# A decoder block's first stage: x turned by products with a diagonal, weights loaded ahead of parameters, units interleaved by k

## The chip, the cores and the metric

The kernel runs on one core of a Trainium2 chip. Five engines work at the same time, each in the order of its own queue: PE (TensorE, matrix products), DVE (VectorE), ACT (ScalarE), POOL (GpSimd) and SP (SyncE, which issues all loads and stores here). The metric is the time of one execution on the device in microseconds (us), lower is better. Before the change three runs gave 1006.0, 1007.21 and 1008.55 us, so a median of 1007.21 us.

## The reference

One decoder block on x with 1024 positions and 1024 channels, all float32. x is divided by its root mean square per position and scaled by a gain per channel; one large projection feeds two branches (an mLSTM with four heads and a diagonal state-space model, S5), which are gated, merged and projected again. The stage that matters here is the first:

```python
def rmsnorm(x, g):
    xf = x.astype(jnp.float32)
    y = xf * lax.rsqrt(jnp.mean(xf * xf, axis=-1, keepdims=True) + NORM_EPS)
    return (y * g.astype(jnp.float32)).astype(x.dtype)

xn = rmsnorm(h, norm_pre_g[l])
proj = xn @ w_in[l]
u_a, z_a, o_a, i_a, f_a, u_b, z_b, g_pre = jnp.split(proj, split_points, axis=-1)
g = jax.nn.sigmoid(g_pre.astype(jnp.float32)).astype(h.dtype)
```

## The kernel before

Every float32 product of the projections is made of three faster ones: an operand a is split into a high part `ah` (ACT writes it, rounded to fp32r) and a low part `al` = a - ah (DVE or POOL), and `dot3` (L179 to L182) adds `ah.bh`, `ah.bl` and `al.bh` in one bank of PSUM. For the weights, `split_w` (L133) does this: `wr` is the raw tile of a load, `wh` and `wl` its parts (L140, L142). For x the parts are `xh[k]` and `xl[k]`, one pair for each of the eight blocks k of 128 channels, with the channels on partitions and the 1024 positions along the row; `HS[0]` and `HS[1]` are the two halves of 512 positions.

x arrives with positions on partitions, in eight tiles `xt` of 128 positions. So it must be normalised and turned. `norm_x` (L266) does the first: ACT squares and sums a row (L269), POOL forms the mean plus epsilon and raises it to the power -1/2 (L270, L271), DVE multiplies the tile with it in place (L272). Turning is a PE transpose against the identity, 128x128 at a time: for the first half of positions eight banks `pts[0]` to `pts[7]`, one for each k, receive four tiles each (L342); for the second half `trans_x` (L279) takes one bank for each k. `evac_x` (L274) then writes `xh` (ACT, times the gain `gpre`) and `xl` (DVE).

A unit is one block of 128 output channels by 512 positions: 24 products into one bank, over k = 0 to 7. `g_unit(i, m, hf)` computes the gates, and tanh of the bank goes to `tg` on ACT and from there to memory. The first stage runs g_unit(0, 0, 0) and g_unit(0, 1, 0), turns the second half, and runs g_unit(0, 0, 1) and g_unit(0, 1, 1). Then the eight `ub` units follow. PSUM has two groups of banks, `pp` (3, for units) and `pm` (5, `mbank()`); the eight `pts` take all of them, so the first unit's bank is that of `pts[0]` and comes free only when `xh[0]` and `xl[0]` have been written.

The order on each engine is the order in which the Python code issues instructions. What sets it here:

- Loads on SP: four x tiles, seven small loads of parameters into `prow` (gain, convolution, head gain and others, L326), the first weights (`fetch()`), four x tiles. Each load uses one of eight semaphores in turn, so the ninth waits for the first to land, the tenth for the second, and so on.
- `pump()` takes raw weights that have been fetched and issues their split; `take(key)` hands a split pair to a unit and pumps the next one ahead. So `take(("g", 0))` in the first unit also issues the split of the weights for `ub` 0, ahead of that unit's tanh.
- 24 transposes of the identity (L334) run on PE before the first tile is ready; nobody reads what they write.

Of the kernel before, what the change touches and what calls it, by code (L numbers as in the profile page):

```python
# [36 lines left out]
def hybrid_block(ctx, tc, x, norm_pre_g, w_in, conv_w, conv_b, w_q, w_k, w_v, b_i, b_f, head_g,  # L37
# [227 lines left out]

    def norm_x(t, xt):  # L266
        s = ssx[:, t:t + 1]
        jk = xp.tile([P, D], F32, tag="junk", bufs=2, name="junk")
        A.activation(jk, xt, AF.Square, accum_out=s)  # L269
        PL.tensor_scalar(s, s, 1.0 / D, EPS, op0=ALU.mult, op1=ALU.add)  # L270
        PL.tensor_tensor(s, s, halfm[:, 0:1], op=ALU.pow)  # L271
        V.tensor_scalar(xt, xt, s, None, op0=ALU.mult)  # L272

    def evac_x(hf, k, pt):  # L274
        A.activation(xh[k][:, HS[hf]], pt, AF.Copy, scale=gpre[:, k:k + 1])
        V.scalar_tensor_tensor(xl[k][:, HS[hf]], pt, gpre[:, k:k + 1],  # L276
                               xh[k][:, HS[hf]].bitcast(F32), op0=ALU.mult, op1=ALU.subtract)

    def trans_x(hf, k, xts):  # L279
        pt = mbank()  # L280
        for t in range(4):
            PE.transpose(pt[:, t * P:(t + 1) * P], xts[t][:, k * P:(k + 1) * P], ident)
        evac_x(hf, k, pt)


    def spill_tanh(o, dst):
# [1 line left out]
        A.activation(t, o, AF.Tanh, scale=0.5)  # L288
# [23 lines left out]


    xts = [load_x(t) for t in range(4)]
    NPAR = 72
    prow = xp.tile([NPAR, P], F32, tag="prow", bufs=1, name="prow")
    r0 = 0
    for src, n in ((norm_pre_g, 8), (conv_w, 32), (conv_b, 8), (head_g, 8), (skip_a, 8), (b_glu, 4),
                   (D_skip, 4)):
# [12 lines left out]
    pts = [bank() if k < 3 else mbank() for k in range(KT)]
    for i in range(24):
        PE.transpose(pts[i % 4][:, :P], ident, ident)  # L334
    for t in range(4):
        norm_x(t, xts[t])
        if t == 3:
            pt = pts[7][:, 3 * P:3 * P + NPAR]
            PE.transpose(pt, prow, ident[:NPAR, :NPAR])
            V.tensor_copy(par, pt)  # L340
# [2 lines left out]
    hg, sk, bgl, dsk = par[:, 48:56], par[:, 56:64], par[:, 64:68], par[:, 68:72]
    pump(lambda: [evac_x(0, k, pts[k]) for k in range(2)])
    for k in range(2, KT):
        evac_x(0, k, pts[k])
    V.tensor_scalar(par[:, 48:64], par[:, 48:64], 0.25, None, op0=ALU.mult)
# [1109 lines left out]
```

## Time and profile before

| what | value |
| --- | --- |
| runs | 1006.0, 1007.21, 1008.55 us |
| the profiled execution | 1006.37 us |
| its span from the first to the last instruction | 1004.3 us |
| mean granted clock of PE | 0.993 |
| PE, DVE, ACT, POOL busy | 976.7, 615.5, 351.1, 154.6 us |
| share of PE in the chain that ended last | 83% |
| products `pp<-xh,wh` at L180, 128x512 | 768, 401 ns each by the records |

The profiled execution's time is 2.1 us more than the span, which lies around it. A row of the timeline holds the start in us, the duration in us, the engine, the line, the operation, the tile written and those read, the shape and the count; in brackets stands how long the engine sat idle before, and what ended that. Products are pipelined: the records of two in succession overlap, and the distance of their starts is what one costs. A row of the windows holds the stretch, then busy time and count of PE, PE's weight loads, DVE, ACT and POOL, the granted clock of PE, the share of the DMA engines and GB/s. In the page's table of 40 slices PE is busy 7 tenths in the first slice, 9 or more in 38, and 7 in the last; the clock is 8 tenths in the first slice and 9 or more in the others.

### The profile page before, as it was taken

What the parts mean: (1) busy time and instruction counts of PE and PEld (TensorE: products, weight loads), DVE (VectorE), ACT (ScalarE), POOL (GpSimd) and SP (SyncE); (2) the same over time, 40 slices, a digit from 0 to 9 for tenths busy, and PEclk for the clock granted to TensorE, in tenths of its full rate; (3) what the DMA queues carried; (4) which work ended last, traced back from release to release, by engine and by line L of the source; (5) the groups of instructions that cost most, each with busy time, mean ns of one, the idle gap of its engine ahead of it and who ended that gap; (6) DMA issues with size and microseconds to landing.
All of it is one profiled execution on the core that took longest, in us unless ns stands there. A gap on an engine that the chain in (4) does not pass through costs nothing.

```text
span 1004.3 us, 15220 instructions
## 1 busy us (share of the span) xinstructions
PE 976.7 (97%) x5617; PEld 840.9 (84%) x5617; DVE 615.5 (61%) x1400; ACT 351.1 (35%) x696; POOL 154.6 (15%) x210
## 2 busy tenths in 40 slices
PE   7999999999999999999999999999999999999997
PEld 6888888788778788978988899889987888779997
DVE  4426496686952854254677477747774888675226
ACT  7322131233032531223544355435543452223311
POOL 4001000000000000012112232223221311343001
PEclk8999999999999999999999999999999999999999
DMA  7344221333056447314433354336436796783504
GB/s 253 94 153 157 90 95 36 93 111 109 17 177 187 170 156 253 107 42 126 138 121 131 95 174 131 135 86 184 132 121 215 248 318 202 271 301 118 189 1 168
DMA packets 115449, 148.31 MB, mean 148 GB/s; under 512 B 19080, under 2 KB 71472, under 8 KB 115376
## 3 DMA queue, kind: packets, MB, share of 16 engines
q1 hardware_dynamic: 115376, 147.35, 45.7%
q8 instruction: 44, 0.72, 0.3%
q14 instruction: 29, 0.24, 0.1%
HBM read 100.88 MB, written 46.43 MB: 147 GB/s over the span
## 4 chain that ended last, share of the span: by engine, by line
PE 83%; DVE 10%; DMA 3%; issue 2%; ACT 1%; SPq 0%; POOL 0%; DVEq 0%; POOLq 0%; ACTq 0%
PE pp L180 22%; PE pp L182 22%; PE pp L181 22%; PE pm L182 4%; PE pm L180 4%; PE pm L181 3%; DVE wl L142 1%; PE pm L1084 1%; DMA wr<-in_w_in_dram 1%; DVE zt L439 1%; PE pm L1007 1%; DMA xt<-in_x_dram 1%; DMA ft<-t_d 1%; PE pm L661 1%; DVE ec_r L439 1%
## 5 line engine op out<-in xcount | busy, mean ns | idle before, releaser
L180 PE MATMUL pp<-xh,wh 128*128 128x512 f32 x768 | 307.6, 401 | 3.2 <-DVE xl L276 2.4
L182 PE MATMUL pp<-xh,wl 128*128 128x512 f32 x768 | 305.0, 397 | 4.4 <-DVE wl L142 4.4
L181 PE MATMUL pp<-xl,wh 128*128 128x512 f32 x768 | 304.7, 397 | 0.0
L182 PEld LDWEIGHTS pp<-xh,wl 128*128 128x128 f32 x768 | 145.0, 189 | 41.0 <-DVE wl L142 6.2
L180 PEld LDWEIGHTS pp<-xh,wh 128*128 128x128 f32 x768 | 145.0, 189 | 39.3 <-DVE xl L276 2.7
L181 PEld LDWEIGHTS pp<-xl,wh 128*128 128x128 f32 x768 | 145.1, 189 | 32.7
L142 DVE TENSOR_TENSOR wl<-wr,wh 128x1024 fp32r<-128x1024 f32 (+2 forms) x71 | 83.4, 1211 | 46.3 <-ACT wh L140 41.7
L140 ACT ACTIVATE wh<-wr 128x1024 fp32r<-128x1024 f32 (+2 forms) x76 | 73.2, 1008 | 40.8 <-PE pm L181 30.7
L182 PE MATMUL pp<-wh,ml 128*128 128x256 f32 x256 | 72.8, 284 | 0.5 <-POOL ml L1363 0.5
L180 PE MATMUL pp<-wh,mh 128*128 128x256 f32 x256 | 72.9, 285 | 0.0
L180 PE MATMUL pp<-wh,xh 128*128 128x256 f32 (+1 forms) x256 | 72.0, 281 | 0.0
L181 PE MATMUL pp<-wl,mh 128*128 128x256 f32 x256 | 71.9, 281 | 0.0
L288 ACT ACTIVATE tg<-pp 128x512 f32<-128x512 f32 x32 | 19.1, 599 | 151.1 <-PE pp L182 75.2
L181 PE MATMUL pp<-wl,xh 128*128 128x256 f32 (+1 forms) x256 | 71.8, 280 | 0.0
L182 PE MATMUL pp<-wh,xl 128*128 128x256 f32 (+1 forms) x256 | 71.8, 280 | 0.0
L182 PEld LDWEIGHTS pp<-wh,ml 128*128 128x128 f32 x256 | 48.1, 188 | 0.7 <-POOL ml L1363 0.7
L181 PEld LDWEIGHTS pp<-wl,mh 128*128 128x128 f32 x256 | 48.6, 190 | 0.1
L180 PEld LDWEIGHTS pp<-wh,mh 128*128 128x128 f32 x256 | 48.4, 189 | 0.2 <-ACT mh L1362 0.2
L181 PEld LDWEIGHTS pp<-wl,xh 128*128 128x128 f32 x256 | 48.2, 188 | 0.2
L180 PEld LDWEIGHTS pp<-wh,xh 128*128 128x128 f32 x256 | 48.1, 188 | 0.2
L182 PEld LDWEIGHTS pp<-wh,xl 128*128 128x128 f32 x256 | 48.0, 187 | 0.0
L981 POOL TENSOR_TENSOR hll<-t2k,hlh 128x512 fp32r<-128x512 f32 x16 | 20.8, 1297 | 166.2 <-ACT hlh L980 89.4
(395 smaller groups left out, 1731.5 us busy)
## 6 DMA issues: line engine op xcount, KB each, us to landing
wr<-in_w_in_dram SPq DMA_DIRECT2D x48, 512.0 KB
t_d<-tg SPq DMA_DIRECT2D x32, 256.0 KB
xt<-in_x_dram SPq DMA_DIRECT2D x8, 512.0 KB
aux<-t_d SPq DMA_DIRECT2D x16, 256.0 KB
gb_d<-aux SPq DMA_DIRECT2D x16, 256.0 KB
so_d<-sow SPq DMA_DIRECT2D x32, 128.0 KB
sz_d<-t2k SPq DMA_DIRECT2D x16, 256.0 KB
cs_d<-t2k SPq DMA_DIRECT2D x16, 256.0 KB
```

The lines of the kernel that those rows point to most:

```text
L140: A.activation(hi, raw, AF.Copy)
L142: eng.tensor_tensor(wl[:, k0:k0 + n, c0:c0 + w], raw, hi.bitcast(F32), op=ALU.subtract)
L180: PE.matmul(o, lh, rh, start=first, stop=False)
L181: PE.matmul(o, lh, rl, start=False, stop=False)
L182: PE.matmul(o, ll, rh, start=False, stop=last)
L288: A.activation(t, o, AF.Tanh, scale=0.5)
L439: V.tensor_tensor(o, a, b, op=op)
L661: PE.matmul(o[NS * b2:NS * (b2 + 1), g * P:(g + 1) * P], q["wt"][:, ri, g, NS * b2:NS * (b2 + 1)], ut[b][:, 2 * g + b2, :], start=True, st ...
L981: PL.tensor_tensor(lo, acc, hi.bitcast(F32), op=ALU.subtract)
L1007: PE.matmul(pm[:, 256 * k:256 * k + 256], wt[:, e, 256 + P * k:256 + P * k + P], wt[:, e, 0:256], start=e == 0, stop=e == 1)
L1084: PE.matmul(sc[:, :P], k_[:, m, sl], q_[:, m, sl], start=m == 0, stop=m == 1)
```

## The change

In `norm_x` the tile itself is left as it is. The mean moves from POOL to DVE, and DVE writes a diagonal `dg` (identity times 1/rms, 128x128) in place of the scaled tile. The turn becomes a true float32 product `xt.T @ dg` (`turn_x`), which turns and scales at once. One tile of the first four (t = 2) is squared on DVE.

The gain gets a load of its own, `grow`, and its own transpose; it and the first weights are loaded ahead of the second four x tiles and of the other parameters, whose transpose comes after both pairs of units. The first weights are split by hand, in pieces of two, two and four blocks of k. More dummy transposes (`warm`) are issued: 30 ahead, and 2, 2 and 10 behind the tiles 0, 1 and 2.

The units of a half run as a pair (`g_pair`): two banks, k by k, six products for each k. The turning of the second half lies among them, and the norms of the second four tiles among the writing of `xh` and `xl`. The split of the next weights (`pump()`) comes after both pairs.

```diff
-    def norm_x(t, xt):
+    def norm_x(t, xt, vec):
...
-        A.activation(jk, xt, AF.Square, accum_out=s)
-        PL.tensor_scalar(s, s, 1.0 / D, EPS, op0=ALU.mult, op1=ALU.add)
+        if vec:
+            V.scalar_tensor_tensor(jk, xt, 1.0, xt, op0=ALU.mult, op1=ALU.mult, accum_out=s)
+        else:
+            A.activation(jk, xt, AF.Square, accum_out=s)
+        V.tensor_scalar(s, s, 1.0 / D, EPS, op0=ALU.mult, op1=ALU.add)
         PL.tensor_tensor(s, s, halfm[:, 0:1], op=ALU.pow)
-        V.tensor_scalar(xt, xt, s, None, op0=ALU.mult)
+        dgs[t] = xp.tile([P, P], F32, tag="dg", bufs=8, name="dg")
+        V.tensor_scalar(dgs[t], ident, s, None, op0=ALU.mult)
+
+    def turn_x(pt, xt, t, k):
+        PE.matmul(pt[:, (t % 4) * P:(t % 4 + 1) * P], xt[:, k * P:(k + 1) * P], dgs[t], start=True, stop=True)
...
+    def g_pair(i, hf, before):
+        tick()
+        wh, wl = cur["g"]
+        o = [bank(), bank()]
+        steps = [(0, 0), (0, 1), (1, 0), (1, 1)] + [(m, k) for k in range(2, KT) for m in range(2)]
+        for m, k in steps:
+            if m == 0:
+                before(k)
+            mc = slice(m * P, (m + 1) * P)
+            dot3(o[m], wh[:, k, mc], wl[:, k, mc], xh[k][:, HS[hf]], xl[k][:, HS[hf]], k, k == 0, k == KT - 1)
+        for m in range(2):
+            g_done(i, m, hf, o[m])
...
     xts = [load_x(t) for t in range(4)]
+    SY.dma_start(grow, norm_pre_g[0].rearrange("(k p) -> k p", p=P))
+    fetch()
+    xts2 = [load_x(t) for t in range(4, 8)]
...
-    fetch()
-    xts2 = [load_x(t) for t in range(4, 8)]
...
-    for i in range(24):
-        PE.transpose(pts[i % 4][:, :P], ident, ident)
+    warm(30)
     for t in range(4):
-        norm_x(t, xts[t])
+        norm_x(t, xts[t], t == 2)
+        if t == 1:
+            PE.transpose(pts[7][:, 3 * P:3 * P + KT], grow, ident[:KT, :KT])
+            V.tensor_copy(gpre, pts[7][:, 3 * P:3 * P + KT])
         for k in range(KT):
-            PE.transpose(pts[k][:, t * P:(t + 1) * P], xts[t][:, k * P:(k + 1) * P], ident)
+            turn_x(pts[k], xts[t], t, k)
+        if t < 3:
+            warm((2, 2, 10)[t])
...
+    A.activation(wh[:, 0:2], ra[:, 0:2], AF.Copy)
+    A.activation(wh[:, 2:4], ra[:, 2:4], AF.Copy)
+    sub(V, slice(0, 2), ra[:, 0:2])
+    for k in range(KT):
+        evac_hi(0, k, pts[k])
+        evac_lo(0, k, pts[k])
+        if k == 1:
+            sub(V, slice(2, 4), ra[:, 2:4])
+            A.activation(wh[:, 4:8], rb, AF.Copy)
+            sub(PL, slice(4, 8), rb)
+        if k >= 3 and k < 7:
+            norm_x(k + 1, xts2[k - 3], False)
+    pending.append(fetch)
+    g_pair(0, 0, lambda k: k < 6 or trans_x(1, k - 6, xts2))
+    g_pair(0, 1, lambda k: k > 5 or trans_x(1, k + 2, xts2))
+    pump()
+    pt = mbank()[:, :NPAR]
+    PE.transpose(pt, prow, ident[:NPAR, :NPAR])
+    V.tensor_copy(par, pt)
...
-    run(unit(lambda: g_unit(0, 0, 0)))
-    run(unit(lambda: g_unit(0, 1, 0)))
-    for k in range(KT):
-        trans_x(1, k, xts2)
-    for m in range(2):
-        run(unit(lambda: g_unit(0, m, 1)))
     prep.close()
```

Three places in the engines' order show what moved. First, PE in the prologue. Before, from the third tile's transposes to the first product of a unit (L342 the transposes of a tile, L339 that of the parameters, L180 a unit's product):

```order
L342 MATMUL pp<-ident,xt 128x128 x3
L342 MATMUL pm<-ident,xt 128x128 x5
L339 MATMUL pm<-ident,prow 128x72
L342 MATMUL pp<-ident,xt 128x128 x3
L342 MATMUL pm<-ident,xt 128x128 x5
L180 MATMUL pp<-xh_96,wh 128x512
```

Now, from behind tile 0's products to tile 3's (L281 the products with `dg`, L368 the dummies, L374 the transpose of the gain):

```order
L368 MATMUL pp<-ident 128x128 x2
L374 MATMUL pm<-ident,grow 128x8
L281 MATMUL pp<-dg,xt 128x128 x3
L281 MATMUL pm<-dg,xt 128x128 x5
L368 MATMUL pp<-ident 128x128 x2
L281 MATMUL pp<-dg,xt 128x128 x3
L281 MATMUL pm<-dg,xt 128x128 x5
L368 MATMUL pp<-ident 128x128 x3
L368 MATMUL pm<-ident 128x128 x4
L368 MATMUL pp<-ident 128x128 x3
L281 MATMUL pp<-dg,xt 128x128 x3
L281 MATMUL pm<-dg,xt 128x128 x5
```

Dummies and the gain's transpose now stand between the tiles, ten of them between tile 2 and tile 3; the parameters' transpose has moved to behind both pairs.

Second, DVE from its first instruction to the first low part of x (L275 the mean, L278 the diagonal, L272 the square of tile 2, L389 a weight split, L287 a low part). Now:

```order
L275 TENSOR_SCALAR ssx<-ssx 128x1
L278 TENSOR_SCALAR dg<-ident,ssx 128x128
L375 COPY par<-pm 128x8
L272 SCALAR_TENSOR_TENSOR junk,ssx<-xt 128x1024
L275 TENSOR_SCALAR ssx<-ssx 128x1
L278 TENSOR_SCALAR dg<-ident,ssx 128x128
L275 TENSOR_SCALAR ssx<-ssx 128x1
L278 TENSOR_SCALAR dg<-ident,ssx 128x128
L389 TENSOR_TENSOR wl<-wr,wh 128x512
L287 SCALAR_TENSOR_TENSOR xl_104<-pp,par,xh_96 128x512
```

Before, there stood four scalings of a tile, the copy of all parameters, a whole weight split and then the first low part; the copy of the gain now stands ahead of tile 2's square.

Third, ACT around the end of the stage (L140 the high part of weights, L269 a Square, L288 or L300 the tanh of a gate unit, L275 or L284 a high part of x, L374 or L429 the copy of a `ub` unit). Before:

```order
L269 ACTIVATE junk,ssx<-xt 128x1024 x4
L140 ACTIVATE wh<-wr 128x1024 x2
L288 ACTIVATE tg<-pp 128x512 x2
L275 ACTIVATE xh_96<-pm,par 128x512
L275 ACTIVATE xh_97<-pm,par 128x512
```

Now:

```order
L284 ACTIVATE xh_102<-pm,par 128x512
L284 ACTIVATE xh_103<-pm,par 128x512
L300 ACTIVATE tg<-pp 128x512 x2
L140 ACTIVATE wh<-wr 128x1024 x4
L429 COPY uc<-pp 128x8x64 x4
```

The two high parts of the weights for `ub` 0 stood ahead of the first pair's tanh; now they are the first two of the four behind the second pair's tanh.

More of the change, by code (lines that the diff above doesn't have):

```diff
@@ L264, in load_x, with evac_hi, evac_lo @@
         return xt
-    def norm_x(t, xt):
+    dgs = {}
+    def norm_x(t, xt, vec):
         s = ssx[:, t:t + 1]
         jk = xp.tile([P, D], F32, tag="junk", bufs=2, name="junk")
[L269 to L274, printed above, removed]
+        if vec:
[3 more added lines that the diff above has]
+        V.tensor_scalar(s, s, 1.0 / D, EPS, op0=ALU.mult, op1=ALU.add)
+        PL.tensor_tensor(s, s, halfm[:, 0:1], op=ALU.pow)
+        dgs[t] = xp.tile([P, P], F32, tag="dg", bufs=8, name="dg")
+        V.tensor_scalar(dgs[t], ident, s, None, op0=ALU.mult)
+    def turn_x(pt, xt, t, k):
+        PE.matmul(pt[:, (t % 4) * P:(t % 4 + 1) * P], xt[:, k * P:(k + 1) * P], dgs[t], start=True, stop=True)
+    def evac_hi(hf, k, pt):
         A.activation(xh[k][:, HS[hf]], pt, AF.Copy, scale=gpre[:, k:k + 1])
+    def evac_lo(hf, k, pt):
         V.scalar_tensor_tensor(xl[k][:, HS[hf]], pt, gpre[:, k:k + 1],
@@ L281, in trans_x @@
         for t in range(4):
-            PE.transpose(pt[:, t * P:(t + 1) * P], xts[t][:, k * P:(k + 1) * P], ident)
-        evac_x(hf, k, pt)
+            turn_x(pt, xts[t], 4 * hf + t, k)
+        evac_hi(hf, k, pt)
+        evac_lo(hf, k, pt)
     def spill_tanh(o, dst):
@@ L291, in hybrid_block, with g_done @@
     cur = {}
+    def g_done(i, m, hf, o):
+        ct = 2 * i + m
+        dst = (t1_d if ct < 8 else t2_d)[(ct % 8) * P:(ct % 8 + 1) * P, HS[hf]]
+        spill_tanh(o, dst)
+    def g_pair(i, hf, before):
[10 more added lines that the diff above has]
+            g_done(i, m, hf, o[m])
     def g_unit(i, m, hf):
@@ L297, in g_unit @@
         proj_cm(o, cur["g"], m * P, xh, xl, HS[hf])
-        ct = 2 * i + m
-        dst = (t1_d if ct < 8 else t2_d)[(ct % 8) * P:(ct % 8 + 1) * P, HS[hf]]
-        spill_tanh(o, dst)
+        g_done(i, m, hf, o)
     def zb_unit(i, m, hf):
@@ L314, in hybrid_block @@
     xts = [load_x(t) for t in range(4)]
-    NPAR = 72
+    grow = xp.tile([KT, P], F32, tag="grow", bufs=1, name="grow")
+    SY.dma_start(grow, norm_pre_g[0].rearrange("(k p) -> k p", p=P))
+    fetch()
+    xts2 = [load_x(t) for t in range(4, 8)]
+    NPAR = 64
     prow = xp.tile([NPAR, P], F32, tag="prow", bufs=1, name="prow")
     r0 = 0
-    for src, n in ((norm_pre_g, 8), (conv_w, 32), (conv_b, 8), (head_g, 8), (skip_a, 8), (b_glu, 4),
-                   (D_skip, 4)):
+    for src, n in ((conv_w, 32), (conv_b, 8), (head_g, 8), (skip_a, 8), (b_glu, 4), (D_skip, 4)):
         src = src[0]
@@ L327, in hybrid_block, with warm @@
         r0 += n
-    fetch()
-    xts2 = [load_x(t) for t in range(4, 8)]
-    par = main.tile([P, 80], F32, name="par")[:, 0:NPAR]
-    gpre, cw, cb = par[:, 0:8], par[:, 8:40].rearrange("p (j k) -> p j k", j=4), par[:, 40:48]
+    par = main.tile([P, 80], F32, name="par")
+    gpre, par = par[:, 64:72], par[:, 0:NPAR]
+    cw, cb = par[:, 0:32].rearrange("p (j k) -> p j k", j=4), par[:, 32:40]
+    hg, sk, bgl, dsk = par[:, 40:48], par[:, 48:56], par[:, 56:60], par[:, 60:64]
     pts = [bank() if k < 3 else mbank() for k in range(KT)]
-    for i in range(24):
-        PE.transpose(pts[i % 4][:, :P], ident, ident)
+    def warm(n):
+        for i in range(n):
+            PE.transpose(pts[i % 7][:, 3 * P:], ident, ident)
@@ L335, in hybrid_block @@
+    warm(30)
     for t in range(4):
-        norm_x(t, xts[t])
[L337 to L340, printed above, removed]
-        for k in range(KT):
-            PE.transpose(pts[k][:, t * P:(t + 1) * P], xts[t][:, k * P:(k + 1) * P], ident)
[L343 to L346, printed above, removed]
@@ L347, in hybrid_block @@
-    V.tensor_scalar(par[:, 48:64], par[:, 48:64], 0.25, None, op0=ALU.mult)
-    V.tensor_scalar(bgl, bgl, 0.5, None, op0=ALU.mult)
-    for t in range(4):
-        norm_x(t + 4, xts2[t])
-    run(unit(lambda: g_unit(0, 0, 0)))
-    run(unit(lambda: g_unit(0, 1, 0)))
-    for k in range(KT):
-        trans_x(1, k, xts2)
-    for m in range(2):
-        run(unit(lambda: g_unit(0, m, 1)))
+        norm_x(t, xts[t], t == 2)
+        if t == 1:
+            PE.transpose(pts[7][:, 3 * P:3 * P + KT], grow, ident[:KT, :KT])
+            V.tensor_copy(gpre, pts[7][:, 3 * P:3 * P + KT])
@@ new lines, in hybrid_block, with sub @@
+        for k in range(KT):
+            turn_x(pts[k], xts[t], t, k)
+        if t < 3:
+            warm((2, 2, 10)[t])
+    key, kt, ncol, raws = raw_q.popleft()
+    wh = wp.tile([P, kt, ncol], F32R, tag="wh", name="wh")
+    wl = wp.tile([P, kt, ncol], F32R, tag="wl", name="wl")
+    ra, rb = raws[0][2], raws[1][2]
+    cur["g"] = (wh, wl)
+    assert key == ("g", 0)
+    def sub(eng, ks, raw):
+        eng.tensor_tensor(wl[:, ks], raw, wh[:, ks].bitcast(F32), op=ALU.subtract)
+    A.activation(wh[:, 0:2], ra[:, 0:2], AF.Copy)
@@ L357, in hybrid_block @@
+    pump()
+    pt = mbank()[:, :NPAR]
+    PE.transpose(pt, prow, ident[:NPAR, :NPAR])
+    V.tensor_copy(par, pt)
+    V.tensor_scalar(par[:, 40:56], par[:, 40:56], 0.25, None, op0=ALU.mult)
+    V.tensor_scalar(bgl, bgl, 0.5, None, op0=ALU.mult)
     prep.close()
```

## The prediction

> **What bounds the kernel now.** I read the page's busy table first, then the chain that ended last, then the first 50 us piece by piece.
>
> ```profile
> PE 976.7 (97%) x5617; PEld 840.9 (84%) x5617; DVE 615.5 (61%) x1400; ACT 351.1 (35%) x696; POOL 154.6 (15%) x210
> ```
>
> PE (TensorE) is busy 97% of the 1004.3 us span and the chain of waits lies on it for 83%. The change touches only the start, and everything behind it (DVE's work on the S5 parameters too) is released by PE in program order. So a microsecond at which the first `ub` unit starts later is a microsecond of time; I see nothing later that would absorb it. The question is when that unit starts and runs on, now and then. The chain in order of time begins thus:
>
> ```profile
> 2.16 6.21 DMA xt<-in_x_dram
> 8.38 4.00 DMA wr<-in_w_in_dram
> 12.40 1.07 ACT wh L140
> 13.49 1.23 DVE wl L142
> 14.72 0.67 DVE xl L276
> 15.44 0.79 PE pp L180
> ```
>
> The fourth x tile lands at 8.38, only then are the first weights issued, they land at 12.40, are split in two steps, and PE's first product starts at 15.44. The windows give the granted clock (the last figure but two of a row):
>
> ```profile
> 14.00:15.00 1.00, 0.00 (x0) 0.00 (x0) 1.00 (x2) 1.00 (x3) 0.00 (x0) 0.87 1.01 410
> 21.00:22.00 1.00, 1.00 (x4) 0.76 (x4) 0.75 (x1) 1.00 (x5) 0.72 (x2) 0.72 0.34 115
> ```
>
> During PE's pause the clock falls to half (from the 0.87, at about 14.7), and it comes back at about 21.6 (the 0.72). PE's own rows show the price and the ends of the stage:
>
> ```profile
> 15.44 0.79 PE L180 MATMUL pp<-xh,wh 128*128 128x512 f32 x1 [2.42 <-DVE xl L276]
> 29.51 2.76 PE L282 MATMUL pm<-ident,xt 128*128 128x128 f32 x23
> 33.45 0.47 PE L180 MATMUL pp<-xh,wh 128*128 128x512 f32 x1
> 44.50 0.39 PE L182 MATMUL pp<-xh,wl 128*128 128x512 f32 x1
> 44.73 0.40 PE L180 MATMUL pp<-xh,wh 128*128 128x512 f32 x1
> ```
>
> From 33.45 to 44.73, 48 products take 11.28 us (0.235 each). The same 48 of the first half take 14.07 us (15.44 to 29.51), so the cold clock costs 2.8 us. The 32 transposes between take 3.94 us (0.123 each). At 44.73 the `ub` unit follows without a gap.
>
> **The change, part by part.** *Turning by a product.* A float32 product of 128x128 by 128x128 occurs at L701 and L702; each shows as two records:
>
> ```profile
> 177.98 0.40 PE L182 MATMUL pp<-xh,wl 128*128 128x512 f32 x1
> 178.21 0.39 PE L701 MATMUL pm<-ut,m 128*128 128x128 f32 x2
> 181.56 0.39 PE L702 MATMUL pm<-ss__1532,vs 128*128 128x128 f32 x2
> ```
>
> From the first start to the last lie 15 products in 3.35 us: 0.223 each. So the 32 of the second half cost 7.14 us on PE, where 32 transposes cost 3.94: **+3.2 us**. They lie between products of the units, but PE does one thing at a time, so nothing hides them.
>
> *When the first product starts.* Tile 0 before:
>
> ```profile
> 4.58 1.06 ACT L269 ACTIVATE junk<-xt 128x1024 f32<-128x1024 f32 x1 [2.52 <-DMA xt<-in_x_dram]
> 5.82 0.19 POOL L270 TENSOR_SCALAR ssx<-ssx 128x1 f32<-128x1 f32 x1 [4.40 <-ACT junk L269]
> 5.86 1.06 ACT L269 ACTIVATE junk<-xt 128x1024 f32<-128x1024 f32 x1
> 6.09 0.55 POOL L271 TENSOR_TENSOR ssx<-ssx,halfm 128x1 f32<-128x1 f32 x1
> 6.68 0.75 DVE L272 TENSOR_SCALAR xt<-xt,ssx 128x1024 f32<-128x1024 f32 x1 [6.68 <-POOL ssx L271]
> 20.13 0.17 DVE L347 TENSOR_SCALAR par<-par 128x16 f32<-128x16 f32 x1
> ```
>
> The mean now runs on DVE, a small instruction as at 20.13 (0.17); the power stays (0.55). The diagonal, 128 wide, lies between 0.17 (16 wide) and 0.75 (1024 wide); on a line between them 0.23. With the old hand-overs of 0.05 to 0.08 it is ready at 6.9. Tile 0's eight products run from 6.95 to 8.73, two dummies and the transpose of the gain row end at 9.06 (this row, queued right behind the fourth x tile, should land near 8.4), tile 1's products at 10.84, two more dummies at 11.05. Tile 2's square is on DVE, behind the gain copy that waits for that transpose: 9.3, copy 0.2, then a 1024-wide instruction with two inputs (1.23, as wl L142 above), mean, power and diagonal about 1.05: ready at 11.8. Its products run from 11.85 to 13.63. Then the **ten dummies** (0.107 each, from the pitch of the warm ones: 4.59 to 5.02 is four) stand in PE's queue ahead of tile 3 until 14.7, although tile 3's diagonal is ready at 12.9, one such chain behind tile 2's. Tile 3's first product ends its bank at about 15.1.
>
> ```profile
> 4.59 0.27 PE L334 MATMUL pm<-ident 128*128 128x128 f32 x1
> 5.02 0.27 PE L334 MATMUL pm<-ident 128*128 128x128 f32 x1
> 30.20 4.73 ACT L275 ACTIVATE xh<-pm,par 128x512 fp32r<-128x512 f32 x8
> 30.92 5.36 DVE L276 SCALAR_TENSOR_TENSOR xl<-pm,par,xh 128x512 fp32r<-128x512 f32 x8 [2.45 <-ACT xh L275]
> ```
>
> ACT's high part takes 0.59 to 0.65, DVE's low part 0.67 to 0.75, and the first product waits for both, since it takes over that bank: it starts at **16.65, 1.2 us later** than before. The weights no longer matter there: issued sixth and seventh, they follow the fourth x tile (8.38) at the tiles' pace (1.28, from the Squares at 4.58 and 5.86) and land near 9.7 and 11; ACT has split them long before 16. My bounds for this start are 15.8 (tile 2 at once behind the two dummies) and 17.2.
>
> *The clock.* PE has no pause above 0.9 us between 1.4 and 16.6, so the clock stays up: **-2.8 us**. That the dummies lift it is seen at once: two starts lie 0.213 apart early on (2.11 to 2.32) and 0.11 from 4.59.
>
> ```profile
> 2.11 0.42 PE L334 MATMUL pm<-ident 128*128 128x128 f32 x1
> 2.32 0.85 PE L334 MATMUL pp<-ident 128*128 128x128 f32 x3
> ```
>
> The Trainium skill, page "TensorE: Matmul & The Clock Gate", Part 4 on the PE-mode transpose, speaks against this: transposes are said not to count as busy for the clock. By it the dummies would be idle time, the clock would rise only through the products, and the time would be that of the fourth rival below. The trace disagrees: at 4.59 nothing but transposes had run.
>
> *Units interleaved by k.* The same 96 products. DVE must make xl0 to xl6 (4.7), half a weight split (0.65) and four diagonals, each with a chain of about 1.1 behind a Square on ACT, before the second half's turning can start: from 15.9 to about 26.1. PE has done k = 0 to 5 of both units (36 products, 8.4) at 25.1 and three of the four products at 25.75: **+0.4 us** of waiting, between 0 and 1.2. Eight changes between the two kinds of product add 0 to 0.7; I take 0, since the passage from 177.98 to 178.21 above is no longer than between two unit products. SP's moved loads cost nothing: the parameters are needed after both pairs, when they have lain there for 25 us.
>
> *The split of the next weights.* Before, ACT's wh for `ub` 0 stood ahead of both tanh and hidden under unit products. Now `pump()` comes after both pairs: on ACT, in order, wh of `ub` 0 stands behind the last tanh, which waits for PE's last product; PE's next product waits for wh, and the third one for DVE's wl. Before, the same sequence runs at this place for `ub` 1, which PE did not wait for:
>
> ```profile
> 44.98 0.60 ACT L288 ACTIVATE tg<-pp 128x512 f32<-128x512 f32 x1 [5.05 <-PE pp L182]
> 45.48 1.05 ACT L140 ACTIVATE wh<-wr 128x1024 fp32r<-128x1024 f32 x1
> 46.56 1.23 DVE L142 TENSOR_TENSOR wl<-wr,wh 128x1024 fp32r<-128x1024 f32 x1 [3.47 <-ACT wh L140]
> ```
>
> wh done 46.53, wl 47.79. PE's slot was 44.73; two products (0.47) fit in between; the third waits until 47.8: 3.07 - 0.47 = **+2.6 us** (2.0 to 3.2). Behind it PE's whole queue waits, and all that PE releases. The second half of the split is ready before k = 4. The parameters' transpose adds 0.1.
>
> *Sum.* Start +1.2, clock -2.8, turning +3.2, diagonals +0.4, late split +2.6, parameters +0.1: **+4.7**. The profiled execution took 1006.37 us, 0.84 under the median of the runs shown, 1007.21. So 1006.37 + 4.7 = 1011.1. All the terms' bounds together give 1009.2 to 1013.7.
>
> **The rivals.** *The new wait also drops the clock.* The trace shows it later:
>
> ```profile
> 299.99 0.46 PE L702 MATMUL pm<-ss__2622,vs 128*128 128x128 f32 x2 [1.31 <-DVE ss__2622 L439]
> 301.40 0.72 PE L702 MATMUL pm<-ss__2622,vs 128*128 128x128 f32 x2 [0.73 <-DVE ss__2622 L439]
> 301.00:302.00 1.00, 0.60 (x3) 0.63 (x4) 0.97 (x3) 0.00 (x0) 0.00 (x0) 0.73 0.00 0
> 304.00:305.00 1.00, 1.00 (x8) 1.00 (x6) 0.00 (x0) 0.00 (x0) 0.00 (x0) 0.57 0.20 68
> ```
>
> Pauses of 1.31 and 0.73 us, 2.0 together, were followed by half clock from 301.46 to 304.86: 3.4 us, of which half is lost. The new wait has about 1.7 and 0.6. Against it: these two pauses did nothing,
>
> ```profile
> 867.26 0.50 PE L182 MATMUL pp<-xh,wl 128*128 128x512 f32 x1 [0.99 <-DVE wl L142]
> 869.49 0.50 PE L182 MATMUL pp<-xh,wl 128*128 128x512 f32 x1 [1.27 <-DVE wl L142]
> ```
>
> since they are 2.2 us apart; it depends on where the pauses fall. 1011.1 + 1.6 = 1012.7. The Trainium skill, same page, Part 1, lets the clock fall only after at least one idle window of some 3.4 us; by that rule this rival is impossible and 1011.1 stands. The trace disagrees: 1.31 was the longest pause there.
>
> *The late split is hidden.* Only if ACT got to wh ahead of the tanh; its order speaks against. 1011.1 - 2.6 = 1008.5.
>
> *Not slower: the product costs what the transpose costs.* It decides at 0.123 a piece. Then the second half saves 3.2, and the start comes 1.45 earlier, as each tile ends 0.8 sooner and dummies and diagonals follow at their pace: 15.2. 1011.1 - 4.65 = 1006.4, no change. L701 speaks against. With the split hidden as well it would be 1003.8, faster.
>
> *The dummies do not hold the clock*, so that the change does not do what it says: products from 6.95 at half speed for up to 6.8 us (14.7 to 21.6 above lasted as long), 3.4 us of progress less the 0.8 of pause, so 2.6 more: 1013.7.
>
> **How the numbers follow.** My forecast 0.46, clock drop 0.27, split hidden 0.10, cheap products 0.08, cold dummies 0.06, both savings 0.03. A measurement of this kernel can tell about 0.3%, 3 us, from no change, so slower begins at 1010.2. Of my forecast's own 1009.2 to 1013.7 a fifth lies below that (0.09). Slower: 0.37 + 0.27 + 0.06 = 0.70; same: 0.09 + 0.10 + 0.08 = 0.27; faster 0.03. The range takes in the cheap product and the clock drop with some of its bounds: 1006.3 to 1014.0; outside lie the two savings together and the upper edges.
>
> **What would show it.** In the new trace: first unit product at 16.65 with a granted clock of 1.00; the products at L281 in pairs of records, 0.22 each; a wait for DVE's `dg` below 1.2 us near 25; the first `ub` product near 48.4, waiting for ACT's wh, and the third near 49.5, waiting for DVE's wl. I am wrong if L281 shows 0.12, if the ten dummies end before tile 2's successor is ready, or if PE passes from the second pair to `ub` without a gap.

## The result and the profile after

| kernel | runs | median (range), us | recorded ratio to before, 95% interval |
| --- | --- | --- | --- |
| before | 4 | 1007.69 (1006.0 to 1008.55) | |
| after | 4 | 1012.61 (1012.41 to 1012.81) | 1.0065 (1.0045 to 1.0085) |
| the same two on a second chip: before | 25 | 1005.62 (1001.84 to 1011.67) | |
| after | 4 | 1013.49 (1011.98 to 1014.95) | 1.0095 (1.0072 to 1.0118) |

The recorded ratio is not the ratio of the two medians, which is 1.0049 on the first chip and 1.0078 on the second; both of these lie within the intervals. The change makes the kernel slower by 0.5 to 1.2% if both intervals are taken together. The profiled execution of after took 1012.41 us, its span is 1010.3 us: 6.0 more than the 1004.3 of before. The forecast was 4.7 more. First the page's busy table and clock row of after:

```profile
PE 984.6 (97%) x5702; PEld 849.8 (84%) x5702; DVE 614.4 (61%) x1412; ACT 351.2 (35%) x695; POOL 150.9 (15%) x202
...
PEclk9999999999999999999999999999999999999999
```

PE is busy 8 us more, and the clock's first slice, 8 tenths in before, is 9 or more. PE's timeline of after, through the first stage:

```profile
7.29 0.38 PE L368 MATMUL pp<-ident 128*128 128x128 f32 x2
7.50 0.83 PE L281 MATMUL pp<-dg,xt 128*128 128x128 f32 x6
12.36 0.94 PE L281 MATMUL pp<-dg,xt 128*128 128x128 f32 x6 [0.34 <-DVE ssx L275]
14.25 0.49 PE L368 MATMUL pp<-ident 128*128 128x128 f32 x3
15.34 0.83 PE L281 MATMUL pp<-dg,xt 128*128 128x128 f32 x6
17.29 0.50 PE L180 MATMUL pp<-xh,wh 128*128 128x512 f32 x1
25.79 1.35 PE L281 MATMUL pm<-dg,xt 128*128 128x128 f32 x8
26.90 0.48 PE L180 MATMUL pp<-xh,wh 128*128 128x512 f32 x1
28.39 1.05 PE L281 MATMUL pm<-dg,xt 128*128 128x128 f32 x8
29.19 0.48 PE L180 MATMUL pp<-xh,wh 128*128 128x512 f32 x1
29.51 0.40 PE L181 MATMUL pp<-xl,wh 128*128 128x512 f32 x1
47.30 0.27 PE L408 MATMUL pm<-ident,prow 64*128 64x64 f32 x1
49.05 0.50 PE L180 MATMUL pp<-xh,wh 128*128 128x512 f32 x1 [1.48 <-ACT wh L140]
50.31 0.50 PE L182 MATMUL pp<-xh,wl 128*128 128x512 f32 x1 [0.53 <-DVE wl L142]
```

The reader sees in order: 30 dummies that end at 7.50; ten dummies ahead of tile 3 (14.25 to 15.34); the first unit product at 17.29 (15.44 before); groups of four turning products, two records each, that take 0.80 and make the next product's step 0.32 in place of 0.23; and, where before PE ran on into `ub` without a gap, two waits for its weights. The third `ub` product starts at 50.31. Before it started at 45.20:

```profile
45.20 0.40 PE L182 MATMUL pp<-xh,wl 128*128 128x512 f32 x1
```

So 5.1 of the 6.0 us are there at 50 us.

What ACT and DVE did at that place, from their timelines:

```profile
46.72 1.34 ACT L300 ACTIVATE tg<-pp 128x512 f32<-128x512 f32 x2 [2.82 <-PE pp L182]
47.95 1.99 ACT L140 ACTIVATE wh<-wr 128x1024 fp32r<-128x1024 f32 x2
49.03 2.36 DVE L142 TENSOR_TENSOR wl<-wr,wh 128x1024 fp32r<-128x1024 f32 x2 [4.35 <-ACT wh L140]
```

ACT had been idle for 2.82 us and started on wh only behind both tanh, as the order said.

The other 0.9 us arise in the last S5 block, where ACT's tanh waits for a store to free its buffer. From the waits of ACT between 250 and 300 us (in total, times, longest), the row of before and that of after, and PE's wait further on in after:

```profile
ACT tg L288 <- DMA t_d<-tg: 15.1, 1, 15.1
...
ACT tg L300 <- DMA t_d<-tg: 16.1, 1, 16.1
...
306.24 0.46 PE L757 MATMUL pm<-ss__2656,vs 128*128 128x128 f32 x2 [2.34 <-DVE ss__2656 L494]
```

The tanh comes 1 us later, and so does what hangs on it, down to PE's wait for DVE's `ss`: 2.34 us, 1.31 in this profile of before. The experiments below say whose that microsecond is.

### The profile page after: what moved, and what is told of

Same layout as the page of the kernel before. It is cut to its first block, busy times and chain, and to the rows that moved or that the text cites. A ratio compares the mean times of both kernels' runs of the same rounds, so it can differ in the third digit from the quotient of the medians.

```text
span 1010.3 us, 15392 instructions
## 1 busy us (share of the span) xinstructions
PE 984.6 (97%) x5702; PEld 849.8 (84%) x5702; DVE 614.4 (61%) x1412; ACT 351.2 (35%) x695; POOL 150.9 (15%) x202
## 4 chain that ended last, share of the span: by engine, by line
PE 81%; DVE 10%; DMA 3%; issue 2%; ACT 2%; SPq 1%; POOL 1%; DVEq 0%; POOLq 0%; ACTq 0%
PE pp L180 21%; PE pp L182 21%; PE pp L181 21%; PE pm L182 4%; PE pm L180 3%; PE pm L181 3%; DVE wl L142 1%; PE pm L1139 1%; PE pm L281 1%; DVE zt L494 1%; PE pm L1062 1%; DMA xl<-yl_d 1%; DMA t_d<-tg 1%; PE pm L716 1%; DMA ft<-t_d 1%
## 5 line engine op out<-in xcount | busy, mean ns | idle before, releaser
L180 PE MATMUL pp<-xh,wh 128*128 128x512 f32 x768 | 307.0, 400 | 2.2 <-ACT wh L140 1.5
L180 PEld LDWEIGHTS pp<-xh,wh 128*128 128x128 f32 x768 | 144.3, 188 | 37.5 <-ACT wh L140 1.6
L140 ACT ACTIVATE wh<-wr 128x1024 fp32r<-128x1024 f32 (+2 forms) x74 | 71.1, 1006 | 44.5 <-PE pm L181 30.8
L180 PE MATMUL pp<-wh,mh 128*128 128x256 f32 x256 | 72.9, 285 | 0.0
L180 PE MATMUL pp<-wh,xh 128*128 128x256 f32 (+1 forms) x256 | 72.0, 281 | 0.0
L300 ACT ACTIVATE tg<-pp 128x512 f32<-128x512 f32 x32 | 19.0, 598 | 141.7 <-PE pp L182 67.2
L180 PEld LDWEIGHTS pp<-wh,mh 128*128 128x128 f32 x256 | 48.4, 189 | 0.3 <-ACT mh L1417 0.2
L180 PEld LDWEIGHTS pp<-wh,xh 128*128 128x128 f32 x256 | 48.0, 188 | 0.2
```

The costliest lines, as they stand in the source:

```text
L140: A.activation(hi, raw, AF.Copy)
L180: PE.matmul(o, lh, rh, start=first, stop=False)
```

## A second measure: the granted clock of every run

The times of the kernel before spread over 10 us on one chip, and each run lists its mean granted clock (rounded to 0.001, which is 1 us). The two go together: of 31 runs of before the slowest two, 1011.8 and 1011.53, had 0.989, and the fastest, 1001.0, had 0.999. A straight line through the 31 gives 0.89 us for each 0.001, and the runs lie about 1.0 us off it, where they lie 2.5 us off their mean (standard deviations). So I use time x clock beside the times, as an estimate of what a run would take at full clock. It also counts half speed as lost that lies in a pause of PE, where it costs nothing, so I estimate that it comes out about 1 us too low for before, which has the most of it: the windows of the first profile count about 3.4 us as lost between 10 and 25 us, and e5 below gets back 2.28. Time x clock and the loss in the table are means over the runs. The kernels of a group shared a chip and its runs of before; each group is another chip, and before alone came out at 1000.7, 999.9 and 1000.3 by time x clock:

| kernel | runs | median | ratio to before, 95% interval | time x clock | lost to the clock |
| --- | --- | --- | --- | --- | --- |
| after, first chip | 4 | 1012.61 | 1.0065 (1.0045 to 1.0085) | 1008.8 | 3.8 |
| before, group 1 | 31 | 1005.75 | | 1000.7 | 5.7 |
| e1, split early | 10 | 1009.42 | 1.0034 (1.0014 to 1.0053) | 1006.3 | 3.8 |
| e2, no ten dummies | 10 | 1011.6 | 1.0048 (1.0027 to 1.0069) | 1008.3 | 3.7 |
| e3, second half by transposes | 10 | 1012.12 | 1.0057 (1.0031 to 1.0083) | 1008.0 | 4.0 |
| e5, before with dummies | 10 | 1005.13 | 0.9989 (0.9966 to 1.0012) | 1001.0 | 4.2 |
| before, group 2 | 25 | 1005.62 | | 999.9 | 5.4 |
| e0, after again | 4 | 1013.49 | 1.0095 (1.0072 to 1.0118) | 1008.4 | 5.1 |
| e6, weights ahead | 10 | 1004.61 | 0.9989 (0.9966 to 1.0011) | 1000.2 | 4.5 |
| e7, loads alone | 10 | 1003.58 | 0.9994 (0.9979 to 1.0009) | 1000.0 | 3.9 |
| e8, mended | 10 | 1007.68 | 1.0019 (0.9997 to 1.0041) | 1002.0 | 4.3 |
| before, group 3 | 17 | 1004.53 | | 1000.3 | 5.1 |
| e9, best | 12 | 1003.81 | 0.9982 (0.9961 to 1.0002) | 999.4 | 4.0 |

And from the profiles, the two places that bound the first stage:

| profile | first unit product | third `ub` product | between |
| --- | --- | --- | --- |
| before; b1; b2 (the same kernel) | 15.44; 15.25; 15.94 | 45.20; 43.80; 45.51 | 29.76; 28.55; 29.57 |
| after; e0; a1 (the same kernel) | 17.29; 16.89; 16.86 | 50.31; 49.91; 49.86 | 33.02; 33.02; 33.00 |
| e1 | 16.76 | 47.54 | 30.78 |
| e2 | 15.55 | 48.57 | 33.02 |
| e3 | 17.06 | 48.70 | 31.64 |
| e5 | 15.38 | 42.92 | 27.54 |
| e6 | 14.83 | 42.37 | 27.54 |
| e7 | 14.22 | 42.37 | 28.15 |
| e8 | 16.09 | 43.70 | 27.61 |
| e9 | 14.20 | 41.60 | 27.40 |

## The experiments

**e1: is the late split a term of its own?** One edit to after: the split is issued among the last pair's steps.

```diff
-    g_pair(0, 1, lambda k: k > 5 or trans_x(1, k + 2, xts2))
-    pump()
+    g_pair(0, 1, lambda k: trans_x(1, k + 2, xts2) if k < 6 else k > 6 or pump())
```

> The changed kernel with one move: the split of the weights for ub 0 is issued ahead of k = 6 of the second pair, so ahead of its tanh on ACT. Theory (the late split is a wait of its own): wh is made near 44, PE goes from the second pair to ub with only the parameters' transpose between, and the third ub product starts near 47.8 in place of 50.31; 1012.6 - 2.5 = 1010.1 us. Rival (PE would wait at this place anyway, for the tanh or for a bank): the third product stays near 50.3 and the time at 1012.6.

ACT's and PE's timelines of e1:

```profile
43.26 2.00 ACT L140 ACTIVATE wh<-wr 128x1024 fp32r<-128x1024 f32 x2
46.18 1.34 ACT L300 ACTIVATE tg<-pp 128x512 f32<-128x512 f32 x2 [0.92 <-PE pp L182]
46.97 0.50 PE L180 MATMUL pp<-xh,wh 128*128 128x512 f32 x1
47.54 0.40 PE L182 MATMUL pp<-xh,wl 128*128 128x512 f32 x1
```

wh now runs ahead of the tanh and PE waits for nothing. From the first unit product to the third `ub` product 30.78 us go by instead of 33.02: the late split cost 2.24 in the trace, and 2.1 to 2.5 by time x clock (1006.3 against 1008.4 and 1008.8; 2.9 if e1 and e0 are each set against before on their own chip, 5.6 and 8.5 above it).

**e2: what do the ten dummies do?** After without them (`warm((2, 2, 0)[t])` for `(2, 2, 10)`).

> The changed kernel without the ten dummy transposes behind tile 2. Theory (they stand in PE's way): tile 3's products start at 14.3 in place of 15.34, the first unit product at 16.2 in place of 17.29, the granted clock stays 1.00; 1012.6 - 1.1 = 1011.5 us. Rival (they hold the clock): half clock for 3.4 us or more in the first 25 us, and 1013.2 or more.

PE's timeline of e2:

```profile
13.60 0.83 PE L281 MATMUL pp<-dg,xt 128*128 128x128 f32 x6
15.55 0.50 PE L180 MATMUL pp<-xh,wh 128*128 128x512 f32 x1
```

Tile 3 follows tile 2 at once, the first unit product starts 1.2 to 1.7 us earlier than in the five profiles with the dummies (after, a1, e0, e1, e3), and the granted clock stays at 1.00 for the first 25 us. So the clock did not need the ten dummies; they stood in the way. By time x clock 0.1 to 0.5 us of it is seen at the end. Set against before on its own chip e2 is 7.6 above and e0 8.5, so 0.9, with an error of about 0.5: no contradiction to the 1.2, and no proof of it. Its profiled execution is 4 us slower than after's (1016.61), and the windows show why:

```profile
45.00:50.00 5.00, 2.99 (x11) 1.76 (x10) 2.67 (x6) 3.07 (x4) 0.00 (x0) 0.93 0.50 140
50.00:55.00 5.00, 5.00 (x18) 3.97 (x17) 1.41 (x3) 1.53 (x2) 0.00 (x0) 0.73 0.61 206
875.00:880.00 5.00, 2.75 (x9) 1.79 (x9) 4.97 (x5) 0.00 (x0) 2.23 (x2) 0.87 1.01 348
```

The clock (last figure but two) fell behind the late split's wait: 5 x 0.07 + 5 x 0.27 = 1.7 us lost there, and about as much again near 310, 340 and 880. That is the first rival of the prediction, in a kernel with the same wait.

**e3: what does a turning product cost?** After, but the second half scaled in place and turned by transposes.

```diff
+        if t > 3:
+            V.tensor_scalar(xt, xt, s, None, op0=ALU.mult)
+            return
...
-            turn_x(pt, xts[t], 4 * hf + t, k)
+            PE.transpose(pt[:, t * P:(t + 1) * P], xts[t][:, k * P:(k + 1) * P], ident)
```

> The changed kernel, where the second half's tiles are scaled in place by DVE again and turned by transposes. Theory (a product costs 0.22, a transpose 0.12): 32 turns cost 3.9 us on PE in place of 7.1, but four scalings of 0.75 stand where four diagonals of 0.29 stood, so tile 7 is ready near 28.1 in place of 26.6 and PE waits there 1.8 longer; the third ub product near 48.9 in place of 50.31; 1011.2 us. Rival (on PE the product costs no more than the transpose): only the longer wait is left, 1014.4 us.

PE's timeline of e3:

```profile
25.95 0.54 PE L296 MATMUL pm<-ident,xt 128*128 128x128 f32 x3
28.30 0.33 PE L296 MATMUL pm<-ident,xt 128*128 128x128 f32 x1 [1.81 <-DVE xt L278]
```

The stage is 1.38 shorter (31.64 against 33.02), although PE now waits 1.81 for the last scaled tile where it waited 0.3 for a diagonal. Without that the transposes save 1.38 + 1.81 - 0.3 = 2.9; the prediction had 3.2. The time itself moved less than the runs can tell.

**e5: what did the clock's fall cost before?** Before, with 16 dummy transposes ahead of tile 3.

```diff
         if t == 3:
+            for i in range(16):
+                PE.transpose(pts[i % 7][:, 3 * P:], ident, ident)
```

> The kernel before, with 16 dummy transposes ahead of tile 3's turning and nothing else. Theory (half clock cost the kernel before 2.8 us, and PE's pause caused it): the first unit product still starts near 15.4, since the weights set it, the clock stays 1.00, the first 48 products take 11.3 us in place of 14.1; 1007.7 - 2.8 = 1004.9 us. Rival (dummy transposes do not count for the clock): half clock from 14.7 as before, 1007.7 us.

Windows and timeline of e5:

```profile
15.00:20.00 5.00, 4.62 (x19) 3.45 (x20) 4.53 (x8) 5.00 (x8) 2.41 (x1) 1.00 1.00 360
...
29.45 1.97 PE L282 MATMUL pm<-ident,xt 128*128 128x128 f32 x12 [0.20 <-DVE xl L276]
42.92 0.39 PE L182 MATMUL pp<-xh,wl 128*128 128x512 f32 x1
```

The clock holds and the third `ub` product comes 2.28 earlier than in the first profile of before. Not 2.8: at full clock PE is ahead of DVE and waits for it in the turning (the 0.20 and some smaller ones), which the slow products had covered; 27.54 us from the first unit product to the third `ub` product, against the 29.76 - 2.8 = 26.96 that the prediction's own products would give. And the median fell by 0.6 only (interval -3.4 to +1.2): the runs of before do not all pay what the first profile showed.

**b1, b2 and a1: the same kernels, profiled again.** Nothing changed, one profile each.

> The kernel before, profiled once more, nothing changed. Theory A (the clock falls or not by the phase of a grid of about 3.4 us against the kernel's pauses): the pauses of PE at 5.7 to 7.5 and 13.0 to 15.4 are there again within 0.3 us, but the drop of the clock behind them may be missing or lie elsewhere; if it is missing, the third product of the first ub unit stands near 42.5 instead of 45.20. Rival B (the pause itself decides): half speed again from about 14.7 to 21.5 and the third ub product at 45.2 again.

> The kernel before, profiled a third time. Theory A (phase): as in b1, with drops at other places than there, or none in the first 25 us. Rival B: the third ub product at 45.2 within 0.3 us. Also read here: how long the tanh of the last S5 block waits for its store (15.06 us in the first profile of before, 15.98 in the run with dummies), which by theory A of the result's last 0.9 us varies by the execution, 15 to 16.5 us, whatever the kernel.

> The changed kernel, profiled once more, nothing changed. Theory A (phase): the wait for the second weights at 47 to 50 us is there again (1.48 and 0.53 us), with or without half speed behind it; the first unit product between 16.6 and 17.3, by when the clock rises under the first dummies. Rival B (the pause itself decides): no drop behind it, as in the first profile of the changed kernel.

The windows from 15 to 25 us of b1, and of b2 behind them:

```profile
15.00:20.00 5.00, 4.75 (x14) 3.80 (x15) 4.87 (x9) 5.00 (x10) 2.44 (x2) 0.67 1.00 351
20.00:25.00 5.00, 5.00 (x22) 4.01 (x22) 2.47 (x6) 5.00 (x9) 4.31 (x8) 0.98 0.28 94
...
15.00:20.00 5.00, 4.06 (x10) 3.19 (x11) 4.87 (x9) 5.00 (x9) 2.39 (x1) 0.50 1.02 391
20.00:25.00 5.00, 5.00 (x20) 4.00 (x19) 2.93 (x7) 5.00 (x10) 3.74 (x7) 0.83 0.37 109
```

The pause ahead of the first product is 2.42, 2.47 and 2.84 us in the three profiles of before; half speed behind it costs 5 x 0.33 + 5 x 0.02 = 1.75 us of clock in b1 and twice that in b2 and in the first profile (0.50 and 0.84 there). So the same pause is followed by about 3.4 us of half speed or by about 6.8. After the same: the rows from 50 to 55 us of after, a1 and e0, all with the same waits of 1.48 and 0.53:

```profile
50.00:55.00 5.00, 4.68 (x20) 3.82 (x21) 1.89 (x6) 0.74 (x1) 0.00 (x0) 1.00 0.83 256
...
50.00:55.00 5.00, 5.00 (x15) 3.92 (x16) 1.63 (x6) 1.06 (x1) 0.00 (x0) 0.66 0.76 228
...
50.00:55.00 5.00, 5.00 (x15) 3.99 (x16) 1.80 (x6) 1.06 (x1) 0.00 (x0) 0.66 0.79 241
```

No fall in the first profile, 5 x 0.34 = 1.7 us lost in the two others (e2 fell too, e3 did not). The same holds later in the kernel. Two pauses of about 0.99 and 1.27 us, 2.2 us apart, lie between 863 and 879 us in all 14 profiles. They did nothing in the first profile of before, as the prediction says, but in b2, the same kernel, where they end at 869.82 and 872.05, they are followed by half speed:

```profile
870.00:875.00 5.00, 3.73 (x10) 2.70 (x11) 4.58 (x5) 0.26 (x1) 0.91 (x1) 0.66 1.03 369
```

That is 5 x 0.34 = 1.7 us again, and so it is in e0, a1, e2 and e7: five of the 14. That an equal pause sometimes drops the clock and sometimes not is shown; that a fixed grid of some 3.4 us decides it, as the expectations say, fits the lengths but was not tried by itself. The Trainium skill, page "TensorE: Matmul & The Clock Gate", Part 1 ("What's actually happening"), says that the clock follows a window of 3413 ns that runs freely and does not start with the kernel, so that the point of change varies from run to run. By that figure, as an estimate, half speed through one window costs 1.7 us and through two 3.4; the losses in the profiles agree (1.7 and 3.4). The store's wait in the last S5 block was 15.06 in the first profile of before alone, and 15.7 to 16.4 in the 13 others, of both kernels and all variants; PE's wait for `ss` behind it was 2.43 and 2.30 in b1 and b2. So the last 0.9 us of the profiles' difference belong to that one execution of before, not to the change.

**e0: after on the other kernels' chip.**

> The changed kernel itself, timed beside the others and the kernel before on one chip. What it is for: every run has its granted clock beside its time, so time x clock gives what the run would take at full clock. Theory A (the change adds about 8 us of work and waits and takes away about 2 us of clock loss): time x clock near 1008.8 us against 1000.7 us before, the mean of 1 - clock near 0.004 against 0.0056 before, median 1011 to 1013. Theory B (the loss is a matter of the clock alone): time x clock within 2 us of the kernel before.

Time x clock is 8.5 us above before (1008.4 against 999.9), the median 7.9. The loss to the clock came out at 5.1, not 4.

**e6 and e7: the loads alone.** e6 is before with `fetch()` moved ahead of the parameters. e7 takes after's loads (the gain's own row, the first weights, the second x tiles, then the parameters with their transpose behind both pairs) and leaves the rest as before, with 8 dummies ahead of tile 2 and of tile 3.

> The kernel before with one edit: the first weights are asked for ahead of the parameters, everything else as it was. Theory A (the start of the first unit product waits for the weights: landed at 12.4 in before, at 9.7 in the changed kernel): first unit product near 14.2 instead of 15.44, third product of the first ub unit earlier by at least that much, time x clock 1.2 us below that of the kernel before, and the pause ahead of the first unit product down from 2.4 us to about 1.3. Rival (the parameters, now behind 1 MB of weights, land later than tile 3 is turned): first unit product at 15.4 or later, and no gain or a loss of up to 1 us.

> The changed kernel's order of loads, its separate row of gains and its late transpose of the parameters, but everything else as before: x scaled on VectorE and turned by transposes, the units one after the other, the weights split where they were; and 8 dummy transposes ahead of tile 2 and of tile 3. Theory A (the loads are the good part of the change, product turning and the late split the bad ones): first unit product near 14.2, clock at 1.00 through the first 25 us, third product of the first ub unit near 41.5 (45.20 before, 50.31 in the changed kernel), time x clock 1.0 to 1.5 us below the kernel before. Rival (the interleaved units are what fills the first stage, and without them the start brings nothing): third product of the first ub unit at 42.4 or later, time x clock as before.

PE's timeline of e6, then of e7:

```profile
12.46 0.25 PE L339 MATMUL pm<-ident,prow 72*128 72x72 f32 x1 [0.90 <-DMA prow<-in_D_skip_dram]
14.83 0.50 PE L180 MATMUL pp<-xh,wh 128*128 128x512 f32 x1 [1.24 <-DVE xl L276]
...
14.22 0.50 PE L180 MATMUL pp<-xh,wh 128*128 128x512 f32 x1 [0.80 <-DVE xl L281]
16.32 0.50 PE L181 MATMUL pp<-xl,wh 128*128 128x512 f32 x1 [0.20 <-DVE xl L281]
```

In e6 the parameters land late, as the rival had it, and eat half of the gain: 14.83. With the gain in a row of its own PE starts at 14.22, as expected, but then waits for xl again, and its third `ub` product is no earlier than in e6 (42.37; 41.5 was expected), since the parameters' transpose now stands ahead of `ub` too: the step there is 0.52 in place of 0.23. Both are 2.8 us ahead of the first profile of before at that place and 1.4 ahead of b1. The medians are 1 and 2 us below that of before, but neither interval excludes 1, and by time x clock (1000.2 and 1000.0 against 999.9) nothing of the earlier start is seen at the end: the gain that was expected there is not shown.

**e8: the three costly places mended.** After with e1's edit, without the ten dummies (and 24 for 30 ahead), and e3's transposes with tile 4's square moved ahead of the first `xh`, so that the scaling is done in time.

```diff
-    warm(30)
+    warm(24)
...
     sub(V, slice(0, 2), ra[:, 0:2])
+    norm_x(4, xts2[0], False)
...
-        if k >= 3 and k < 7:
-            norm_x(k + 1, xts2[k - 3], False)
+        if k >= 3 and k < 6:
+            norm_x(k + 2, xts2[k - 2], False)
```

> The changed kernel with its three costly places mended: the second weights split during the last unit pair instead of behind its tanh, the second half of x scaled and turned by transposes with tile 4's square moved ahead, no dummies ahead of tile 3 and 24 at the start. Theory A (the three places add): first unit product near 15.6 (17.29 in the changed kernel), third ub product near 44 (50.31), time x clock near 1002.5 (1008.8), so within 2 us of the kernel before. Rival (one place hides another, VectorE now being the late one for the second half): third ub product at 46 or later, time x clock at 1004.5 or more.

PE's timeline of e8:

```profile
43.70 0.39 PE L182 MATMUL pp<-xh,wl 128*128 128x512 f32 x1
```

The third `ub` product stands at 43.70 and time x clock at 1002.0: 6.4 to 6.8 us below after. The three places add. What is left against before is within the error of its ratio (1.0019, 0.9997 to 1.0041); by time x clock, on the same chip, it is 2.1.

**e9: the best of it.** e7, with both halves of the first weights split on ACT while it stood idle, ahead of the copies of x, and the second low half on POOL.

```diff
-    pump(lambda: [evac_x(0, k, pts[k]) for k in range(2)])
-    for k in range(2, KT):
+    pump(pl=True)
+    for k in range(KT):
```

> The run with the loads alone, and both halves of the first weights split on ScalarE before x is copied out (ScalarE stood idle there from 10.7 to 12.7), the second low half on GpSimd. Theory A (the start and the clock are what can be had in the first stage): first unit product near 14.2, no gap behind it (0.37 us were left at 16.3), third ub product near 41.7 against 42.37 with the loads alone, 42.9 in the kernel before without its clock drop and 45.20 with it; time x clock about 1 us below the kernel before, the clock's loss 1 to 1.5 us below, so a median 1.5 to 2.5 us lower, ratio near 0.998. Rival (what is won at the start is waited for again later): third ub product as said, but time x clock as in the kernel before, within 0.4 us.

PE's timeline of e9:

```profile
14.20 0.50 PE L180 MATMUL pp<-xh,wh 128*128 128x512 f32 x1 [0.80 <-DVE xl L281]
41.60 0.39 PE L182 MATMUL pp<-xh,wl 128*128 128x512 f32 x1
```

The first product stands at 14.20 with no gap behind it, the third `ub` product at 41.60. The median is 0.7 us lower than before's, the means differ by 2.0, and the ratio 0.9982 (0.9961 to 1.0002) just fails to exclude no change. It is some 9 us below after, which was timed on other chips, and 0 to 4 below before; time x clock is 0.9 lower, with an error of about 0.4.

## Why the prediction was right or wrong, point by point

- **A microsecond at the start is a microsecond of time.** Right for the change itself: the 5.1 us at 50 us are still 5.2 at PE's next wait for `wl` (274.11 before, 279.33 after), and e8 gets back at the end what it gets back at 44. For gains of a microsecond (e2, e6, e7) the runs do not settle it.
- **Turning, +3.2.** Right: two records and 0.80 + 0.09 us for four (28.39 to 29.51, less the 0.23 of a unit product), so 0.223 each; e3 makes it 2.9. The split within it was not as told: a product costs 0.20 within such a series of four, and the passage back to unit products, taken as 0, costs 0.09 each time.
- **Wait for the diagonals, +0.4.** Right: the 0.3 that are left of 1.11 (25.79 to 26.90) when the four products are taken off.
- **Late split, +2.6, parameters +0.1.** Right in mechanism and order of waits, sizes 2.24 (e1) and 0.3 (in e1 0.52 us from the last product's start, 46.45, to the next one's, 46.97, where 0.23 would do).
- **All between the first product and the third `ub` product**, without the clock: forecast 6.3, measured 33.02 - 26.96 = 6.06 by the prediction's own base.
- **Start, +1.2.** Mis-sized: 17.29, 16.89 and 16.86 against 16.65. The ten dummies did delay tile 3, as said (e2). But tile 0's products began at 7.50 in the profile, not at 6.95: the 30 dummies ahead ran at 0.213 each until about 7.1 (until about 4.5 in before's first profile), and then stood in the way although the diagonal was ready at 6.75 (DVE's row: 6.46, 0.29 long). The rows of after:

```profile
5.96 0.85 PE L368 MATMUL pp<-ident 128*128 128x128 f32 x3
6.60 0.85 PE L368 MATMUL pm<-ident 128*128 128x128 f32 x4
```

In e1 the dummies became fast earlier and PE was waiting for the diagonal, at 6.87. The term supposed one time for this change of pace; it varies by the execution.
- **Clock, -2.8.** This is the step that failed: the mechanism is as told, but the term is mis-sized. It took one profile's 2.8 us as what before pays in every execution, and had the changed kernel pay nothing. In the profiled pair that is so. But other executions of before pay less (b1: 28.55 in place of 29.76, so 1.6 over the 26.96), and in the order of the kernel before PE gets back only 2.3 even with a full clock (e5), since DVE is next. And the new wait drops the clock itself, in three of the five profiles that have it, for 1.7. The three profiles of before lie 2.3 us above 26.96 in the mean, and the three of after lose 1.1 in the mean behind the new wait: a saving of 1.2. In the means over all timed runs the loss to the clock is 5.1 to 5.7 for before and 3.8 and 5.1 for after. So the saving is about 1 (0 to 2), not 2.8.
- **The sum.** Forecast 1011.1, measured 1012.61 and 1013.49. The terms without the clock add up to +7.5 in the prediction; the profiles show 6.06 + 1.4 to 1.85 there, so 7.5 to 7.9. With a saving of 1 at the clock that is 6.5 to 6.9, so 1012.9 to 1013.3 from 1006.37. Over the runs the clock's term is what makes most of the difference to the forecast, with 0.2 to 0.6 from the start. In the profiled pair, where the clock paid as forecast, the difference of 1.3 is made up otherwise: 0.65 at the start and 0.9 from before's luck in S5, less 0.24 between. And that the medians of the first chip lie 4.92 apart, close to the 4.7, is in part luck: the four runs of before there have a mean of 1007.5, the three larger groups 1005.4 to 1006.4, and on the second chip the medians lie 7.9 apart.
- **The rivals.** That the new wait drops the clock too, 1012.7, was given a quarter; it and the forecast are two outcomes of one kernel, by execution, not two answers. The reason given against it, that two pauses 2.2 us apart do nothing, does not hold: the same two dropped the clock in b2. That the dummies do not hold the clock and that the product costs a transpose are refuted: from 7.50 on a product at L281 takes 0.22, neither the half speed of the one nor the 0.12 of the other, and the granted clock is 1.00 through 25 us. That the split is hidden happened only in e1 and e8, where it was made so.

## What to carry to other kernels

A drop of the granted clock is to be priced as a chance times about 1.7 or 3.4 us, not by the one profile at hand: two profiles of the same kernel, or the list of clocks of its runs, tell how often it is paid, and each new wait of a microsecond or more adds such a chance. Dummies are worth their place only in a pause that would be there without them; behind a wait that sometimes ends early, they become the wait. And a producer's work for the next unit (here the split of its weights) is to be issued ahead of anything on the same engine that waits for the end of the present one.

## What was not expected of the hardware

- The same kernel on the same chip took from 1001.0 to 1011.8 us, and its listed clock went from 0.999 to 0.989 with it, so that most of the spread goes with the clock. Three profiles of it (the first, b1, b2) show why: half speed falls or does not fall behind the same pauses, and 5.2, 6.9 and 8.6 us are lost in their windows.
- Where the clock falls, the half speed lasts about 3.4 us or twice that: 1.7 us of clock were lost in a window in b1, a1, e0 and e2, and about 3.4 in two profiles of before.
- Nothing but dummy transposes ran first, from 1.4 us on, and they went from 0.213 us start to start to 0.107 at about 4.5 us in one execution and at about 7.1 in another. That this is the clock's rise is read from the halved distance: the windows list a granted clock of 1.00 over the slow stretch too, so the list, and with it time x clock, does not count this start.
- The clock falls behind pauses shorter than the half speed that follows: 2.47 us in b1, 1.48 and 0.53 in a1. The Trainium skill, page "TensorE: Matmul & The Clock Gate", Part 1 ("What's actually happening"), has it fall after at least one idle window of about 3.4 us; no pause of PE in the first 60 us of these profiles is that long, so the measurements disagree with that entry.
